# Moving 56 DMA issues from SyncE's queue to GpSimd's in a one-core hybrid decoder layer

## The chip, the cores and the metric

The kernel runs on one core of one Trainium2 chip. The metric is the device time of one execution in microseconds (us). Two times occur below: the median of three timed runs, and the time of the one execution that the profiler recorded, whose span runs from its first to its last instruction.

## What is computed

One layer is applied to 2048 new prompt tokens and to 8 single-token samples with saved states. In short form:

```
n    = rmsnorm(x)
proj = n @ w_in                      # u_s5 | q,k,v | z | beta, a
y    = gelu(s5_scan(u_s5))           # diagonal state space
gl   = y @ w_glu
y_s5 = gl[:, :512] * sigmoid(gl[:, 512:])          # the output gate
o    = delta_rule(l2norm(silu(conv(q,k,v))), ...)  # 4 delta net heads of 128
y_gdn = rmsnorm(o) * silu(z)
x = x + concat(y_s5, y_gdn) @ w_out
x = x + conv_ffn(rmsnorm(x))         # 1024 -> 2*2816 -> 1024
```

All matmuls of the large products are float32 split in a high and a low part, three products each.

## The kernel before

The 2048 prompt tokens are taken in four quarters of 512 columns (`QT`); quarter 0 also carries the 8 samples as columns 512 to 519. The stages follow each other loosely: norm and the S5 input products, then the S5 batches with the first delta net heads (list `MIXERS`), then from about 510 us the list `FFN`, in which the output gate (`s5_glu`), the rest of the delta net heads, the sample states and the four FFN quarters are interleaved letter by letter. TensorE runs its queue in order through all of it.

The tensor `mixT` in DRAM collects the results of both mixers, 1024 rows by 2056 columns. Rows 0 to 511 are written by the output gate (tile `mo`), rows 512 to 1023 by the heads (tile `zs`, end of `gdn_back`), the samples' columns by small stores. `ffn_mix` loads them again (tile `mr`), eight tiles for each quarter, and splits them into `nT`, the operand of the product with `w_out`; `ffn_res` loads the residual (tile `xr`).

`s5_glu` is called for quarters 0 and 1 and then for 2 and 3. For each of its two quarters it loads four tiles `yr` from `yD` (128 rows, each of 8 pieces of 64 floats) and, in quarter 0, a strip of 8 columns from `ysD`. ScalarE and VectorE split each into `yT`. Then four row blocks `a` follow, each with a weight load, two products, a sigmoid in `sg` and the gated result in `mo`, which is stored to `mixT`.

Three things set the order around these transfers. Each engine's queue is in order, and a DMA issue waits in the queue of the engine that issues it. SyncE (SP) issues nearly all loads and stores: the weights (`wr`, two buffers), the mixers' transfers, the bounce of `gdn_inverse` through `nD` and `xD`. GpSimd (POOL) issues the S5 results (`yD`, `ysD`), the output rows (`yout`), the sample states (`S0s`) and the samples' delta net result (`mixT<-sst`, line 1038), and computes the halos, the low parts of `gt` and the sums of squares. And `yr`, `sg`, `mo`, `zs`, `raw`, `t`, `s`, `mr`, `xr` and others share one pool of nine buffers (`NV = 9`, tag `v`), so a buffer whose store has not landed holds back the next tile of that pool.

The order of each queue is not the order of the source text. It is written at build time by a planner that plays the program through a timeline and gives each instruction a place when it could start there:

```python
TCARGS = dict(schedule_with_timeline_sim=True)
```

Of the kernel before, what the change touches and what calls it, by code (L numbers as in the profile page):

```python
# [20 lines left out]
QT = 512  # L21
NQ = QT + 8
# [35 lines left out]
def ncols(q):  # L58
    return NQ if q == 0 else QT


def blocks(q):
    return [(0, 256), (256, NQ)] if q == 0 else [(0, QT)]
# [6 lines left out]
def split(nc, hi, lo, raw, eng=None):  # L70

    nc.scalar.activation(hi, raw, AF.Copy)  # L72
    (eng or nc.vector).tensor_tensor(lo, raw, f32(hi), op=OP.subtract)  # L73


def sigmoid_(nc, out, x, scale=1.0):

    nc.scalar.activation(out, x, AF.Exp, scale=-scale)
    nc.scalar.activation(out, out, AF.Ln, bias=1.0)
    nc.scalar.activation(out, out, AF.Exp, scale=-1.0)  # L80
# [13 lines left out]
def rsqrt_cols(c, ss, n, scale, tag, rows=128, tmp=None):  # L94

    a, y, t = tmp or [c.sm.tile([128, n], F32, name=tag + s) for s in ("_a", "_y", "_t")]
    a, y, t = a[:rows], y[:rows], t[:rows]
    c.nc.vector.tensor_scalar(a, ss, scale, c.epscol[:rows], op0=OP.mult, op1=OP.add)
    return rsqrt_(c.nc, a, y, t)
# [185 lines left out]
def mm3(nc, out, wh, wl, xh, xl, first, last):  # L285
    nc.tensor.matmul(out, lhsT=wh, rhs=xh, start=first, stop=False)  # L286
    nc.tensor.matmul(out, lhsT=wh, rhs=xl, start=False, stop=False)  # L287
    nc.tensor.matmul(out, lhsT=wl, rhs=xh, start=False, stop=last)  # L288


def wsplit(c, src, eng=None):

    hi, lo, wr = c.W("whi"), c.W("wlo"), c.WR("wr")
    src(wr)
    split(c.nc, hi, lo, wr, eng or c.wl)
    return hi, lo
# [421 lines left out]
def s5_glu(c, q0, yT):  # L718

    nc = c.nc  # L720
    Q = (q0, q0 + 1)
    for i, q in enumerate(Q):
        for kt in range(4):
            rows = slice(kt * 128, kt * 128 + 128)
            yr = c.V("yr")
            nc.sync.dma_start(yr[:, :QT].rearrange("p (j m) -> p j m", j=8), c.yD[rows, :, q * 64:(q + 1) * 64])
            if q == 0:
                nc.sync.dma_start(yr[:, QT:NQ], c.ysD[rows])
            n = ncols(q)
            split(nc, yT[:, 4 * i + kt, 0, :n], yT[:, 4 * i + kt, 1, :n], yr[:, :n])  # L730
    wg = c.inp["s5_w_glu"][0].rearrange("(k p) f -> p k f", p=128)
    for a in range(4):
        v = lambda t: t.rearrange("p (k s f) -> p k s f", k=4, s=2)

        def load(wr):
            for s in range(2):
                nc.sync.dma_start(v(wr)[:, :, s], wg[:, :, s * 512 + a * 128:s * 512 + a * 128 + 128])
        h4, l4 = (v(t) for t in wsplit(c, load))
        for i, q in enumerate(Q):
            sg, mo = c.V("sg"), c.V("mo")  # L740
            for (b0, b1) in blocks(q):
                pab = {}
                for s in (1, 0):
                    p = pab[s] = c.ps("mm")
                    for kt in range(4):
                        K = 4 * i + kt
                        mm3(nc, p[:, :b1 - b0], h4[:, kt, s], l4[:, kt, s], yT[:, K, 0, b0:b1], yT[:, K, 1, b0:b1], kt == 0, kt == 3)
                    if s == 1:
                        sigmoid_(nc, sg[:, b0:b1], p[:, :b1 - b0])
                pa = pab[0]  # L750
                n8 = min(b1, QT) - b0
                j0, j1 = b0 // 64, (b0 + n8) // 64
                nc.vector.tensor_tensor(mo[:, 0:QT].rearrange("p (m j) -> p j m", j=8)[:, j0:j1],
                                        pa[:, :n8].rearrange("p (j m) -> p j m", m=64),
                                        sg[:, b0:b0 + n8].rearrange("p (j m) -> p j m", m=64), op=OP.mult)
                if b1 > QT:
                    nc.vector.tensor_tensor(mo[:, QT:NQ], pa[:, n8:n8 + 8], sg[:, QT:NQ], op=OP.mult)
            nc.sync.dma_start(c.mixT[a * 128:(a + 1) * 128, q * QT:(q + 1) * QT], mo[:, 0:QT])
            if q == 0:
                nc.sync.dma_start(c.mixT[a * 128:(a + 1) * 128, 2048:2056], mo[:, QT:NQ])  # L760
        yield


# [186 lines left out]
def gdn_back(c, q, h, col, F):  # L950

    nc, gp, sm = c.nc, c.gp, c.sm
    S0 = c.Sst[:, h]
    kq, kg, vt, AT, hc, zs, T = F
    ot = gp.tile([128, QT], F32, name="ot", bufs=1).rearrange("p (a b) -> p a b", a=4)
    for ci in range(4):
        sl = slice(ci * 128, ci * 128 + 128)
        pV = c.ps("b")
        nc.tensor.matmul(pV[:, 0:128], lhsT=kq[:, 0, sl], rhs=S0, start=True, stop=True)
        nc.tensor.matmul(pV[:, 128:256], lhsT=kq[:, 1, sl], rhs=S0, start=True, stop=True)  # L960
        rv = gp.tile([128, 128], F32, name="rv", bufs=1)
        nc.vector.scalar_tensor_tensor(rv, pV[:, 0:128], col[:, 6, ci, h:h + 1], vt[:, ci], op0=OP.mult, op1=OP.add)
        nc.scalar.activation(ot[:, ci], pV[:, 128:256], AF.Copy, scale=col[:, 3, ci, h:h + 1])
        nc.tensor.matmul(pV[:, 256:384], lhsT=T[:, ci], rhs=rv, start=True, stop=True)
        vn = gp.tile([128, 128], F32, name="vn", bufs=1)
        nc.vector.tensor_scalar(vn, pV[:, 256:384], hc[:, 5, ci:ci + 1], None, op0=OP.mult)
        pO = c.ps("b")
        nc.tensor.matmul(pO[:, 0:128], lhsT=kg[:, ci], rhs=vn, start=True, stop=True)
        nc.tensor.matmul(pO[:, 128:256], lhsT=AT[:, ci], rhs=vn, start=True, stop=True)
        nc.vector.scalar_tensor_tensor(S0, S0, col[:, 5, ci, h:h + 1], pO[:, 0:128], op0=OP.mult, op1=OP.add)  # L970
        nc.vector.tensor_tensor(ot[:, ci], pO[:, 128:256], ot[:, ci], op=OP.add)

    so = sm.tile([128, 4], F32, name="so")
    for ci in range(4):
        jk = gp.tile([128, 128], F32, name="jk2", tag="rv", bufs=1)
        nc.scalar.activation(jk, ot[:, ci], AF.Square, accum_out=so[:, ci:ci + 1])
    nc.vector.tensor_tensor(so, so, hc[:, 6], op=OP.mult)
    f = rsqrt_cols(c, so, 4, 1.0, "ro")
    nc.vector.tensor_tensor(f, f, hc[:, 1], op=OP.mult)
    for ci in range(4):  # L980
        nc.scalar.activation(ot[:, ci], ot[:, ci], AF.Copy, scale=f[:, ci:ci + 1])
    po = c.ps("b")
    for ci in range(4):
        nc.tensor.transpose(po[:, ci * 128:(ci + 1) * 128], ot[:, ci], c.ident)
    nc.vector.scalar_tensor_tensor(zs[:, :QT], po, c.col1(C_ON), zs[:, :QT], op0=OP.mult, op1=OP.mult)
    nc.sync.dma_start(c.mixT[512 + h * 128:512 + h * 128 + 128, q * QT:(q + 1) * QT], zs[:, :QT])


def gdn_sample(c, col):
# [301 lines left out]
def kernel(tc, inp, outp):  # L1291
# [7 lines left out]
    with ExitStack() as es:  # L1299
# [114 lines left out]
        def rest():  # L1414
            x2 = c.fb.tile([128, 8, NQ], F32, name="x2")
            nT = c.fb.tile([128, 8, 2, NQ], F32R, name="nT2")
            for q0 in (0, 2):
                yield from s5_glu(c, q0, nT)
            xrs, fin = ffn_mix(c, 0, nT), lambda: None
            yield  # L1420
            for q in range(4):
                xrs, fin = yield from ffn(c, q, x2, nT, xrs, fin)
# [35 lines left out]
```

## Time and profile before

| what | value |
|---|---|
| median of three runs | 2814.07 us (2813.53 to 2818.86) |
| the profiled execution's own time | 2812.3 us |
| its span | 2810.5 us |
| TensorE (PE) busy, weight loads (PEld) | 95%, 81% |
| VectorE, ScalarE, GpSimd busy | 76%, 50%, 24% |
| mean granted TensorE clock | 0.975 |
| DMA, hardware queue and software queue | 283.27 MB and 28.61 MB |

The shares are of the span. The execution's own time is 1.8 us longer than the span, and 1.8 us shorter than the median. DMA issues, register and semaphore instructions do not count as busy. The hardware queue is that of SyncE's issues, the software queue that of GpSimd's.

### The profile page before, as it was taken

The page shows a single profiled execution, that of the slowest core. Times are in us where ns is not written, and L with a number is a line of the kernel's source. Part 1 is how long each engine was busy: PE and PEld are TensorE (multiplying, and loading weights), DVE is VectorE, ACT ScalarE, POOL GpSimd, SP SyncE. Part 2 cuts the span into 40 slices and gives each one's busy share as a digit, 9 for nine tenths or more (in the row PEclk, how much of TensorE's full clock was granted, in tenths as well). Part 3 has the DMA queues.
Part 4 walks back from the last instruction along what each step waited for, and adds up shares of the span by engine and source line. Part 5 has one row for each costly group of instructions (what it writes and reads, how often), then busy time and mean ns, then how long its engine had stood idle before and what let it go on. Part 6 is the DMA issues. An engine that isn't in the chain of part 4 may idle for free.

```text
span 2810.5 us, 43010 instructions
## 1 busy us (share of the span) xinstructions
PE 2669.6 (95%) x15216; PEld 2266.6 (81%) x15216; DVE 2134.4 (76%) x4726; ACT 1391.7 (50%) x2806; POOL 661.9 (24%) x940
## 2 busy tenths in 40 slices
PE   5988888899999999998999999999999998999998
PEld 4887776787988999998777878877888787788887
DVE  6678899767778887778598777986868677677776
ACT  4535665554555544444544554544544434444443
POOL 3325431000121122212331111213212222322223
PEclk9998888999999999999999999999999999999999
DMA  7654433454434332333434333344333334443432
GB/s 198 201 155 117 123 104 109 103 129 117 117 85 108 86 96 85 95 92 111 126 97 121 90 92 106 85 133 125 95 100 90 91 93 133 141 119 99 123 116 69
DMA packets 421674, 314.63 MB, mean 112 GB/s; under 512 B 75311, under 2 KB 371672, under 8 KB 421443
## 3 DMA queue, kind: packets, MB, share of 16 engines
q1 hardware_dynamic: 411123, 283.27, 35.2%
q0 software_dynamic: 10336, 28.61, 3.4%
q8 instruction: 120, 1.97, 0.3%
q14 instruction: 95, 0.78, 0.1%
HBM read 264.74 MB, written 47.34 MB: 111 GB/s over the span
## 4 chain that ended last, share of the span: by engine, by line
PE 76%; DVE 13%; DMA 5%; issue 3%; ACT 2%; SPq 1%; POOL 0%; POOLq 0%; ACTq 0%; DVEq 0%
PE psmm L286 17%; PE psmm L287 17%; PE psmm L288 17%; PE psd L286 5%; PE psd L287 5%; PE psd L288 5%; DVE hh L654 1%; DVE wlo L73 1%; DVE tm L911 1%; DVE x L1107 1%; DVE nT L73 1%; DVE x L1197 1%; DVE X L912 1%; PE psf L887 1%; DMA N<-nD 1%
## 5 line engine op out<-in xcount | busy, mean ns | idle before, releaser
L286 PE MATMUL psmm<-nT,whi 128*128 128x512 f32 (+2 forms) x2992 | 1067.3, 358 | 29.8 <-ACT zs L841 8.0
L287 PE MATMUL psmm<-nT,whi 128*128 128x512 f32 (+2 forms) x2992 | 1060.4, 355 | 1.3 <-DVE nT L223 0.8
L288 PE MATMUL psmm<-nT,wlo 128*128 128x512 f32 (+2 forms) x2992 | 1058.0, 354 | 0.4 <-POOL wlo L73 0.4
L72 ACT ACTIVATE whi<-wr 128x1024 fp32r<-128x1024 f32 x372 | 394.0, 1060 | 608.5 <-PE psmm L287 443.9
L286 PEld LDWEIGHTS psmm<-nT,whi 128*128 128x128 f32 x2992 | 569.9, 191 | 109.9 <-ACT zs L841 8.7
L287 PEld LDWEIGHTS psmm<-nT,whi 128*128 128x128 f32 x2992 | 570.4, 191 | 79.1 <-issue 1.7
L288 PEld LDWEIGHTS psmm<-nT,wlo 128*128 128x128 f32 x2992 | 569.8, 191 | 78.9 <-issue 0.9
L73 DVE TENSOR_TENSOR wlo<-wr,whi 128x1024 fp32r<-128x1024 f32 x356 | 445.6, 1253 | 92.4 <-ACT whi L72 89.9
L1107 DVE TENSOR_TENSOR x<-psd,x 128x512 f32<-128x512 f32 (+2 forms) x464 | 257.1, 557 | 144.4 <-PE psd L288 142.6
L286 PE MATMUL psd<-gt,whi 128*128 128x512 f32 (+2 forms) x928 | 323.5, 349 | 16.5 <-DVE x L1107 14.5
L287 PE MATMUL psd<-gt,whi 128*128 128x512 f32 (+2 forms) x928 | 317.2, 342 | 0.0
L288 PE MATMUL psd<-gt,wlo 128*128 128x512 f32 (+2 forms) x928 | 315.3, 341 | 0.0
L1254 DVE SCALAR_TENSOR_TENSOR t<-raw,cc,t 128x512 f32<-128x512 f32 x352 | 270.6, 771 | 14.2 <-ACT t L1251 6.6
L1255 POOL COPY halo<-raw 128x2 f32<-128x2 f32 x176 | 77.4, 440 | 777.9 <-DVE raw L1250 702.2
L286 PEld LDWEIGHTS psd<-gt,whi 128*128 128x128 f32 x928 | 175.2, 189 | 47.2 <-DVE x L1107 22.0
L73 POOL TENSOR_TENSOR gt<-s,gt 128x512 fp32r<-128x512 f32 (+1 forms) x88 | 132.3, 1503 | 321.0 <-ACT gt L72 320.7
L287 PEld LDWEIGHTS psd<-gt,whi 128*128 128x128 f32 x928 | 175.4, 189 | 21.7
L288 PEld LDWEIGHTS psd<-gt,wlo 128*128 128x128 f32 x928 | 174.8, 189 | 20.8
L1250 DVE TENSOR_TENSOR raw<-psmm,rs 128x512 f32<-128x512 f32 (+1 forms) x214 | 123.7, 578 | 67.4 <-PE psmm L288 65.7
L1251 ACT ACTIVATE t<-raw,cc 128x512 f32<-128x512 f32 (+1 forms) x176 | 127.0, 722 | 64.6 <-DVE raw L1250 61.3
L911 DVE TENSOR_TENSOR tm<-X,N 128x124 f32<-128x124 f32 (+30 forms) x496 | 132.4, 267 | 28.9 <-DMA N<-nD 19.8
L1117 POOL TENSOR_TENSOR sq<-sq 128x256 f32<-128x256 f32 (+3 forms) x84 | 96.3, 1146 | 222.2 <-ACT sq L1115 219.6
(493 smaller groups left out, 3542.3 us busy)
## 6 DMA issues: line engine op xcount, KB each, us to landing
wr<-in_ffn_w_up_dram SPq DMA_DIRECT2D x176, 512.0 KB
wr<-in_ffn_w_down_dram SPq DMA_DIRECT2D x88, 512.0 KB
wr<-in_w_in_dram SPq DMA_DIRECT2D x64, 512.0 KB
wr<-in_w_out_dram SPq DMA_DIRECT2D x32, 512.0 KB
xTD<-xT SPq DMA_DIRECT2D x32, 256.0 KB
N<-nD SPq DMA_DIRECT2D x16, 512.0 KB
mr<-mixT SPq DMA_DIRECT2D x32, 256.0 KB
xr<-xTD SPq DMA_DIRECT2D x32, 256.0 KB
```

The source lines that it names most:

```text
L72: nc.scalar.activation(hi, raw, AF.Copy)
L73: (eng or nc.vector).tensor_tensor(lo, raw, f32(hi), op=OP.subtract)
L286: nc.tensor.matmul(out, lhsT=wh, rhs=xh, start=first, stop=False)
L287: nc.tensor.matmul(out, lhsT=wh, rhs=xl, start=False, stop=False)
L288: nc.tensor.matmul(out, lhsT=wl, rhs=xh, start=False, stop=last)
L911: nc.vector.tensor_tensor(m, X[:, :, j:j + 1].to_broadcast(sh), N[:, j:j + 1, j + 1:].to_broadcast(sh), op=OP.mult)
L1107: nc.vector.tensor_tensor(x2[:, j, b0:b1], p, x2[:, j, b0:b1], op=OP.add)
L1117: c.nc.gpsimd.tensor_tensor(acc[0], acc[0], s, op=OP.add)
L1250: nc.vector.tensor_tensor(raw[:, 2 + b0:2 + b1], p, rsB[:, b0:b1], op=OP.mult)
L1251: nc.scalar.activation(t[:, :n], raw[:, 2:2 + n], AF.Copy, scale=w[2])
L1254: nc.vector.scalar_tensor_tensor(t[:, :QT], raw[:, j:j + QT], w[j], t[:, :QT], op0=OP.mult, op1=OP.add)
L1255: nc.gpsimd.tensor_copy(c.halo[:, ch], raw[:, QT:QT + 2])
```

## The change

The issues of four kinds of transfers, and of the small strips that go with two of them, are made by GpSimd. These are 16 loads of `yr` from `yD` with 4 strips from `ysD`, 16 stores of `mo` with 4 strips, and 16 stores of `zs`. Sizes, tiles, buffers and the computing instructions stay as they are.

```diff
             yr = c.V("yr")
-            nc.sync.dma_start(yr[:, :QT].rearrange("p (j m) -> p j m", j=8), c.yD[rows, :, q * 64:(q + 1) * 64])
+            nc.gpsimd.dma_start(yr[:, :QT].rearrange("p (j m) -> p j m", j=8), c.yD[rows, :, q * 64:(q + 1) * 64])
             if q == 0:
-                nc.sync.dma_start(yr[:, QT:NQ], c.ysD[rows])
+                nc.gpsimd.dma_start(yr[:, QT:NQ], c.ysD[rows])
...
-            nc.sync.dma_start(c.mixT[a * 128:(a + 1) * 128, q * QT:(q + 1) * QT], mo[:, 0:QT])
+            nc.gpsimd.dma_start(c.mixT[a * 128:(a + 1) * 128, q * QT:(q + 1) * QT], mo[:, 0:QT])
             if q == 0:
-                nc.sync.dma_start(c.mixT[a * 128:(a + 1) * 128, 2048:2056], mo[:, QT:NQ])
+                nc.gpsimd.dma_start(c.mixT[a * 128:(a + 1) * 128, 2048:2056], mo[:, QT:NQ])
...
-    nc.sync.dma_start(c.mixT[512 + h * 128:512 + h * 128 + 128, q * QT:(q + 1) * QT], zs[:, :QT])
+    nc.gpsimd.dma_start(c.mixT[512 + h * 128:512 + h * 128 + 128, q * QT:(q + 1) * QT], zs[:, :QT])
```

## Rows read from the trace of the kernel before

**Rows 1.** Windows by stage: length, busy time (count) of each engine, clock, DMA.

```profile
422.00:510.00 88.00, 74.72 (x405) 56.69 (x404) 78.77 (x246) 52.83 (x143) 19.33 (x28) 0.84 0.37 105
510.00:700.00 190.00, 178.74 (x1054) 150.08 (x1054) 127.10 (x410) 99.94 (x255) 7.98 (x17) 0.94 0.45 117
700.00:2810.00 2110.00, 2064.75 (x11477) 1750.68 (x11477) 1605.80 (x3166) 1016.73 (x1852) 476.19 (x712) 0.99 0.36 104
```

**Rows 2.** Waits of TensorE: us in total, times, longest.

```profile
PE psmm L286 <- ACT whi L72: 4.8, 3, 3.5
...
PE psd L286 <- ACT whi L72: 1.5, 1, 1.5
...
PE psf L1003 <- DMA S0s<-in_state_gdn_dram: 0.6, 1, 0.6
```

**Rows 3.** Waits in SyncE's queue (SPq), same columns.

```profile
SPq L986 <- DVE zs L985: 43.3, 10, 13.4
...
SPq L758 <- DVE mo L753: 22.5, 5, 6.0
```

**Rows 4.** DMA issues by tile: ns min/median/max, first and last start, last S0s' landing.

```profile
L726 SPq DMA_DIRECT2D yr<-yD x16: 517/546/969, 514.7 to 623.4; - x16
...
L728 SPq DMA_DIRECT2D yr<-ysD x4: 642/650/650, 515.3 to 523.9; - x4
...
L758 SPq DMA_DIRECT2D mixT<-mo x16: 319/328/534, 539.1 to 688.7; - x16
...
L986 SPq DMA_DIRECT2D mixT<-zs x16: 319/338/345, 422.2 to 2357.5; - x16
...
L1220 POOL DMA_DIRECT2D out_dram<-yout x34: 513/540/583, 1339.3 to 2806.3; - x34
...
L996 POOL DMA_DIRECT2D S0s<-in_state_gdn_dram x4: 882/892/929, 613.9 to 627.4; - x4
...
DMA to landing us min/median/max: 3.8/5.3/8.6
```

**Rows 5.** DMA issues of the page: count, KB each, median us to landing.

```profile
out_dram<-yout POOLq DMA_DIRECT2D x32, 256.0 KB, 3.6
```

**Rows 6.** Timeline of SyncE's queue: start, us, line, transfer, count.

```profile
514.70 0.58 SPq L726 DMA_DIRECT2D yr<-yD  x1
...
609.25 3.31 SPq L726 DMA_DIRECT2D yr<-yD  x4
...
683.57 0.45 SPq L1129 DMA_DIRECT2D mr<-mixT  x1
688.65 0.32 SPq L758 DMA_DIRECT2D mixT<-mo  x1
689.02 0.42 SPq L1127 DMA_DIRECT2D mr<-mixT  x1
```

**Rows 7.** Chain that ended last, in order of time: start, us, what.

```profile
515.33 2.81 DMA yr<-ysD
...
520.32 3.55 DMA yr<-ysD
...
613.90 4.73 DMA S0s<-in_state_gdn_dram
...
756.55 4.60 DMA xr<-xTD
```

**Rows 8.** Timeline of TensorE; in brackets the idle time before and what ended it.

```profile
519.01 0.80 PE L286 MATMUL psmm<-nT,whi 128*128 128x256 f32 x2 [1.02 <-ACT nT L72]
...
700.56 0.50 PE L286 MATMUL psmm<-nT,whi 128*128 128x512 f32 x1 [1.89 <-ACT t L825]
...
761.72 0.38 PE L286 MATMUL psmm<-nT,whi 128*128 128x256 f32 x1 [1.55 <-DVE x L1153]
```

**Rows 9.** Windows, sum over sixteen stretches of 10 us that hold zs stores after 700.

```profile
sum 160.00, PE 156.96 PEld 136.63 DVE 117.67 ACT 82.59 POOL 35.81; mean PE 9.81 PEld 8.54 DVE 7.35 ACT 5.16 POOL 2.24
```

**Rows 10.** Timeline of GpSimd's queue, the wait in front of line 1038.

```profile
681.90 0.77 POOL L1038 DMA_DIRECT2D mixT<-sst  x1 [53.65 <-DVE sst L1037]
```

## The prediction, made before the changed kernel was run

> **What bounds the kernel now.** I read the windows by stage first, because the transfers that move all lie behind 422 us: the first `zs` store is issued there and the last at 2357.5 [rows 4]. From 422 to 510 TensorE is busy 74.72 of 88 us, from 510 to 700 (the output gate) 178.74 of 190, from 700 on 2064.75 of 2110 [rows 1]. So 13.3 + 11.3 + 45.3 = 69.9 us of idle TensorE time is all that the change can give back in its stretch, and TensorE work itself is untouched by it. The granted clock is 0.94 in the gate's stage and 0.99 afterwards [rows 1], so there is little in the clock either.
>
> Next come the waits, to see which idle time hangs on DMA. TensorE's waits for a split weight are 4.8 and 1.5 us in all, and it waits 0.6 us for a sample state [rows 2]. SyncE's queue, in contrast, stands 43.3 us in front of `zs` stores and 22.5 us in front of `mo` stores [rows 3]; weight loads are queued behind these. The two views together are the point of this case: SyncE waits a lot, and TensorE almost never notices, since the weights are split ahead of their use.
>
> Then I followed the four places where a moved transfer, or one queued behind it, ends a TensorE wait: the gate's entrance at 515, the sample states at 614, the gate's end at 689 and a residual load at 756 [rows 6 to 8].
>
> **Issue time.** SyncE loses 16 x 0.546 + 4 x 0.65 for `yr`, 16 x 0.328 + 4 x some 0.35 for `mo`, and 16 x 0.338 for `zs`: about 23 us [rows 4]. GpSimd gains them at its own prices. A `yr` load has 128 rows of 8 pieces, as an `S0s` load has, so I take that issue's 0.892 us; a `mo` or `zs` store has 128 plain rows of 2 KB like `yout`, so 0.540 us; for the eight strips also 0.54. That is 14.3 + 17.3 + 4.3 = 36 us. Most of it (some 28 us) falls in the stage in which GpSimd computes 7.98 of 190 us [rows 1], the rest is eleven issues spread over 2110 us of which GpSimd fills 476. That idle time is the cover. Without it each issue would put 0.5 to 0.9 us in front of a halo or a `gt` split. I take 0 for TensorE.
>
> **The entrance of the gate, 515 us.** On SyncE the first `yr` is issued at 514.70 and its strip has landed at 515.33 + 2.81 = 518.14, which is 3.44 us after the first issue [rows 6, 7]. The first products wait for its split, with 1.02 us of TensorE idle [rows 8], and the second pair (520.32 + 3.55) is again on the chain [rows 7], because its buffer comes free late. On GpSimd the nearest row above is the first `S0s` load, which has as many pieces and twice the bytes: 4.73 us [rows 7], so 1.3 us later. The nearest below is a 256 KB `yout` store at 3.6 us [rows 5], 0.2 us later. The pieces are what a `yr` load shares with `S0s`, so I take 1.3 us, twice: +2.6. The bounds are 0 and twice 8.6 - 3.44 us (the slowest of the later `S0s` transfers [rows 4]), about +10.
>
> The Trainium skill, "DMA: Bandwidth & Descriptors", section "Latency and other measured facts", gives a first byte after about 1 us for a GpSimd issue and about 0.6 us for a SyncE issue, which speaks against the change. By it alone the term would be an estimated 2 x 0.4 = +0.8 us in place of +2.6, and the sum below would be 1.8 us lower. No row here separates a first byte from the rest of a transfer.
>
> **The sample states, 614 us.** The second half of the gate issues four `yr` loads at 609.25 [rows 6], and the first `S0s` is issued at 613.90 from the other queue [rows 7]. TensorE waits 0.6 us for it [rows 2], so a later landing is paid in full. After the change the `S0s` data stand behind four `yr` (1.05 MB) in one queue. The 4.73 us of the first 512 KB is 111 GB/s for one queue that shares the engines; two of these were issued together, so up to twice that, 222 GB/s, passed. At 222 GB/s 1.05 MB takes 4.7 us; issued from 609.25 on and with some 1.3 us until data move they are through at about 615.3, 1.4 us after the `S0s` issue, and GpSimd's longer issue of the four (3.6 against 3.31 us) adds 0.3. I take +1.7. The lower bound is 0, if `S0s` is queued first; the upper is all eight `yr` in front, 2.1 MB or +9.4 us.
>
> **The end of the gate, 689 us.** The load of the second `mr` stands in SyncE's queue behind the last `mo` store: the strip before it ends at 684.02, then SyncE waits until 688.65 for `mo` and issues `mr` at 689.02 [rows 6]. ScalarE's splits of these `mr` sit in front of the evacuation of a head's product, and TensorE idles 1.89 us on that at 700.56 [rows 8]. With `mo` in GpSimd's queue, the `mr` loads of quarter 0 can go up to 4.6 us earlier: they need the `mo` of quarter 0 and not the last one. The wait is at most 1.89 us, so -1.9, at worst 0. What is late next is the `mr` buffer itself, which is one of the shared nine.
>
> **The residual at 756 us.** The store of a `zs` holds an `xr` load in SyncE's queue; that load's 4.60 us is on the chain [rows 7] and TensorE idles 1.55 us for it at 761.72 [rows 8]. Moved, it gives up to -1.55, at worst 0.
>
> **The other `zs` stores.** Sixteen stretches around the eleven stores after 700 us show 156.96 of 160 us TensorE busy [rows 9], and half of the missing 3 us is the 1.55 just counted. The last store, at 2357.5, is followed by an `mr` load that depends on it; TensorE has other products then. I take 0 for all, and for the earlier ones too.
>
> **The sum.** 0 + 2.6 + 1.7 - 1.9 - 1.55 = +0.85 us on the profiled execution's own 2812.3, or 2813.2; the median stands 1.8 us above that execution, so 2815 us. The bounds of the four terms alone are -3.5 and +19.
>
> **What the sum leaves out.** The planner writes new queues for all engines from 422 us on, because it times the two issuers differently. The trace of before can't show that order. I take 0 and keep both signs in the rivals.
>
> **Rivals.** *Everything moved is hidden anyway*: the planner keeps TensorE's order and slots cover the later landings; 2814 us. Rows 9 and the small waits of rows 2 speak for it, the two `yr` on the chain [rows 7] against. The Trainium skill, same page, section "Issuing engines are not separate DMA queues", says that issuing from several engines saves only sequencer time, since all run on the same 16 DMA engines; that speaks for this rival.
>
> *Faster, SyncE's queue is what counts*: the 43.3 and 22.5 us of waits [rows 3] no longer hold weights back, all of TensorE's 6.3 us of weight waits [rows 2] go, with the 1.9 and 1.55 above, and the entrance stays covered: -9.8, or 2804 us. Against it: at most 6.3 us of 69.9 hang on weights.
>
> *Slower, a blocked GpSimd queue*: line 1038 holds GpSimd 53.65 us until 681.90 [rows 10]. If it is queued ahead of `mo` stores, each keeps one of the nine shared buffers. Up to four held ones leave enough for `sg`, `mo` and a head's tiles; from the fifth on TensorE runs out, at about 660 us, and stands until 682: +20, or 2834 us. Against it: the planner places an instruction when it could start, and the `mo` are ready earlier.
>
> *Slower, a worse order of the gate and heads*: at the idle share of the stretch before it (13.3 of 88 us [rows 1]) the gate's 190 us would hold 28.7 us of idle instead of 11.3; half of that loss is +8.7, or 2823 us, all of it 2831.
>
> **How the numbers follow.** About 0.2% (5.6 us) is what a measurement of this kernel can tell from no change. The forecast of the sum has 0.30 and the hidden case 0.12, together 0.42 within 0.2%. The freed SyncE queue has 0.25 (faster). The worse order, with the upper bounds of the entrance and of `S0s`, has 0.23 and the blocked queue 0.10, together 0.33 slower. Cases of both signs hold more than half, so the likeliest one's own range is 2809 to 2820; for 8 in 10 it reaches to 2803, just past the freed queue's time, and to 2831, which leaves out the blocked queue and some of either tail.
>
> **What would show it.** Right: GpSimd's issues near 0.9 us for `yr` and 0.54 for the stores; the first `yr` landing 4 to 5 us after its issue; TensorE idle in the gate's stage between 10 and 17 us and its waits at 700 and 761 gone; SyncE's waits for `zs` and `mo` gone and standing in GpSimd's queue. Wrong: a GpSimd wait of tens of us in front of a `mo` store, `raw` or `gt` waiting behind one, or more than 5 us of change in TensorE's idle time after 700, where no moved transfer but `zs` is left; that would be the order and not a transfer.

## The result, and the profile after

The changed kernel takes 2833.29 us in the median (2830.66 to 2836.17), beside 2816.47 us (2813.53 to 2819.46) for the kernel before on the same chip. The ratio is 1.006, with a 95% interval of 1.0048 to 1.0072: 17 us slower, outside the forecast range of 2803 to 2831. The profiled execution's own time is 2836.17 us, its span 2834.4 us, 23.9 us longer than the span of before.

The windows by stage, with the same columns as [rows 1], put the loss in the gate's stage:

```profile
422.00:510.00 88.00, 74.66 (x430) 58.01 (x429) 78.96 (x245) 53.90 (x148) 18.36 (x26) 0.86 0.38 107
510.00:700.00 190.00, 168.11 (x988) 140.71 (x986) 118.12 (x398) 92.32 (x237) 36.76 (x57) 0.90 0.37 103
700.00:2834.00 2134.00, 2090.04 (x11564) 1772.10 (x11562) 1620.55 (x3189) 1029.43 (x1873) 481.48 (x728) 0.99 0.36 105
```

TensorE idles 21.9 us between 510 and 700, where it idled 11.3 us, and the clock there is 0.90 instead of 0.94. Windows of fixed times hold different work in the two kernels, so I cut both traces at the same work. The borders are the first group of sample-state products, the last `mo` store, the last `zs` store and the end; TensorE executes 381 and 382 matmuls in the first piece. First the kernel before:

```profile
618.80:688.70 69.90, 68.38 (x381) 57.34 (x382) 45.91 (x147) 31.32 (x69) 2.53 (x3) 0.93 0.43 117
688.70:2357.50 1668.80, 1635.02 (x9536) 1402.83 (x9535) 1297.76 (x2704) 820.71 (x1552) 346.12 (x545) 0.99 0.36 103
2357.50:2810.50 453.00, 439.70 (x1988) 355.81 (x1986) 314.81 (x472) 201.93 (x310) 130.60 (x169) 0.99 0.38 114
```

Then the changed kernel:

```profile
625.70:710.60 84.90, 73.73 (x382) 60.99 (x383) 45.16 (x147) 33.24 (x71) 11.88 (x18) 0.86 0.45 124
710.60:2378.70 1668.10, 1639.15 (x9536) 1407.01 (x9535) 1298.08 (x2704) 820.87 (x1551) 348.67 (x557) 0.99 0.35 102
2378.70:2834.40 455.70, 440.39 (x1986) 356.58 (x1985) 317.11 (x472) 202.38 (x310) 131.50 (x170) 0.99 0.38 113
```

One piece carries the loss: 84.90 us for what took 69.90. Of these 15.0 us, 9.65 are idle TensorE time (11.17 against 1.52 us) and 5.35 are longer matmuls (73.73 against 68.38 us busy, at a clock of 0.86 against 0.93). The other pieces differ by -0.7 and +2.7 us. The rest of the 23.9 us, 6.9 us, lies ahead of the piece: the first `yr` is issued 4.5 us later (519.18 against 514.70), most of the way to it without any moved transfer (the first is at 422 us), and the way from it to the first `mo` store is 2.6 us longer.

Inside the piece there is one large wait. TensorE's timeline (idle time before an instruction in brackets):

```profile
638.54 0.39 PE L288 MATMUL psmm<-nT,wlo 128*128 128x512 f32 x1
648.75 0.80 PE L959 MATMUL psb<-Sst,kq 128*128 128x128 f32 x2 [9.82 <-DVE ot L971]
```

TensorE waits for the state and output updates of a running delta net head (lines 970, 971), which VectorE (DVE in the rows) makes. VectorE's timeline shows why they are late:

```profile
632.73 0.69 DVE L73 TENSOR_TENSOR nT<-yr,nT 128x512 fp32r<-128x512 f32 x1 [0.29 <-ACT nT L72]
645.57 0.29 DVE L911 TENSOR_TENSOR tm<-X,N 128x124 f32<-128x124 f32 x1 [12.15 <-DMA N<-nD]
...
647.36 0.34 DVE L970 SCALAR_TENSOR_TENSOR Sst<-Sst,col,psb 128x128 f32<-128x128 f32 x1
...
648.41 0.29 DVE L971 TENSOR_TENSOR ot<-psb,ot 128x128 f32<-128x128 f32 x1
```

The first product of the next head's inverse (line 911, the sixth of 16 inverses) stands ahead of them in VectorE's queue and waits 12.15 us for the tile `N`. This tile makes a trip through DRAM: `gdn_inverse` writes four 16 KB blocks to `nD` (line 902) and reads them back as the 512 KB of `N` (line 904). Both are issued by SyncE, and neither is part of the change. The chain that ended last runs through both:

```profile
627.49 8.90 DMA nD<-LT
...
636.54 9.01 DMA N<-nD
```

In the kernel before, the four blocks were issued at 619.28 and `N` at 624.10, 4.8 us later; here 626.13 and 636.54, 10.4 us apart. And in VectorE's queue of before the first product stood behind the head's updates:

```profile
637.59 0.35 DVE L970 SCALAR_TENSOR_TENSOR Sst<-Sst,col,psb 128x128 f32<-128x128 f32 x1 [1.74 <-PE psb L969]
637.85 0.28 DVE L971 TENSOR_TENSOR ot<-psb,ot 128x128 f32<-128x128 f32 x1
638.05 0.28 DVE L911 TENSOR_TENSOR tm<-X,N 128x124 f32<-128x124 f32 x1
```

What travels beside the trip is seen in GpSimd's queue of the changed kernel:

```profile
615.97 0.54 POOL L760 DMA_DIRECT2D mixT<-mo  x1
620.76 1.79 POOL L996 DMA_DIRECT2D S0s<-in_state_gdn_dram  x2 [4.25 <-PE psmm L288]
622.54 3.50 POOL L726 DMA_DIRECT2D yr<-yD  x4
626.03 0.57 POOL L758 DMA_DIRECT2D mixT<-mo  x1
626.59 0.89 POOL L726 DMA_DIRECT2D yr<-yD  x1
```

The second half's `yr` stand behind two sample states, which wait 4.25 us for TensorE. They went 0.9 us after the `mo` store before them (608.32 and 609.25 [rows 6]), and now go 7.1 us after it (615.43), in one burst with the states. The shares of the two queues in the DMA engines follow (queue: packets, MB, share of 16 engines), first for 628 to 636.5 us, then 636.5 to 640, then 640 to 645.6:

```profile
q0 software_dynamic: 660, 2.23, 98.8%
q1 hardware_dynamic: 576, 0.07, 6.3%
...
q0 software_dynamic: 256, 0.86, 101.2%
q1 hardware_dynamic: 1, 0.00, 0.6%
...
q1 hardware_dynamic: 143, 0.52, 43.2%
q0 software_dynamic: 59, 0.18, 14.9%
```

All of `N` (143 packets, 0.52 MB) moves after 640 us, when the software queue has run down; in the 3.5 us after its issue one packet of the hardware queue passed. In the kernel before, the hardware queue had 89.4% of the engines in 621 to 624, the software queue 5.9%.

### The profile page after: what moved, and what is told of

It is laid out like the page before. It is cut to its first block, busy times and chain, and to the rows that moved or that the text cites. A ratio compares the mean times of both kernels' runs of the same rounds, so it can differ in the third digit from the quotient of the medians.

```text
span 2834.4 us, 43024 instructions
## 1 busy us (share of the span) xinstructions
PE 2677.1 (94%) x15216; PEld 2271.9 (80%) x15216; DVE 2135.6 (75%) x4726; ACT 1394.4 (49%) x2806; POOL 694.4 (25%) x996
## 4 chain that ended last, share of the span: by engine, by line
PE 76%; DVE 13%; DMA 5%; ACT 3%; issue 2%; SPq 1%; POOL 0%; POOLq 0%; DVEq 0%; ACTq 0%
PE psmm L286 18%; PE psmm L287 17%; PE psmm L288 17%; PE psd L286 5%; PE psd L287 5%; PE psd L288 5%; DVE hh L654 1%; DVE wlo L73 1%; DVE tm L911 1%; DMA N<-nD 1%; DVE x L1107 1%; DVE nT L73 1%; DVE X L912 1%; ACT whi L72 1%; DMA nD<-LT 1%
```

## The experiments

**Theory.** The second half's `yr`, late and in one burst with the sample states on the software queue, slow the trip of `nD` and `N` on the hardware queue (A). The planner has put VectorE's first product ahead of the head's updates, so TensorE pays for it (B). Both are needed. **Rivals:** the `mo` or `zs` stores, which hold shared buffers longer; the order alone; any single part of the `yr` change.

### Each kind of transfer alone

Each of these kernels is the kernel before with one or two of the diff's parts. First the `yr` loads and their strips:

```diff
-            nc.sync.dma_start(yr[:, :QT].rearrange("p (j m) -> p j m", j=8), c.yD[rows, :, q * 64:(q + 1) * 64])
+            nc.gpsimd.dma_start(yr[:, :QT].rearrange("p (j m) -> p j m", j=8), c.yD[rows, :, q * 64:(q + 1) * 64])
             if q == 0:
-                nc.sync.dma_start(yr[:, QT:NQ], c.ysD[rows])
+                nc.gpsimd.dma_start(yr[:, QT:NQ], c.ysD[rows])
```

> Only the yr loads and their strips move to GpSimd, the stores of mo and zs stay with SyncE. Theory A (the yr loads, queued with the S0s loads, delay a head's bounce nD, N through DRAM, and TensorE stands for it): all of the change's loss is here, +14 to +20 us over before (about 2830 to 2836), with a TensorE wait of 7 us or more for a delta net instruction between 620 and 660 us, and N landing 15 us or more after nD's issue. Theory B (stores waiting in GpSimd's queue hold the shared buffers): less than +6 us here.

Measured: 2833.89 us, ratio 1.0057 (1.0044 to 1.007). The whole loss is here, within the interval. Its trace has the same slow trip (`N` lands 18.6 us after the first `nD` issue) and a wait of the same kind, of 5.96 us where 7 or more was expected; what stood behind the product on VectorE was one more split of the gate's input, and the timelines of VectorE and TensorE read:

```profile
639.85 0.29 DVE L911 TENSOR_TENSOR tm<-X,N 128x124 f32<-128x124 f32 x1 [6.80 <-DMA N<-nD]
...
642.52 0.79 PE L287 MATMUL psmm<-nT,whi 128*128 128x512 f32 x1 [5.96 <-DVE nT L73]
```

Then the stores, alone and together:

```diff
-            nc.sync.dma_start(c.mixT[a * 128:(a + 1) * 128, q * QT:(q + 1) * QT], mo[:, 0:QT])
+            nc.gpsimd.dma_start(c.mixT[a * 128:(a + 1) * 128, q * QT:(q + 1) * QT], mo[:, 0:QT])
...
-    nc.sync.dma_start(c.mixT[512 + h * 128:512 + h * 128 + 128, q * QT:(q + 1) * QT], zs[:, :QT])
+    nc.gpsimd.dma_start(c.mixT[512 + h * 128:512 + h * 128 + 128, q * QT:(q + 1) * QT], zs[:, :QT])
```

> Only the mo stores move to GpSimd. Theory A: between -3 and +2 us; the gate ends at the same place, and the TensorE wait of 1.89 us behind the gate (mr loads queued behind the last mo store) is gone. Theory B: +8 us or more, with tiles of the shared pool (sg, raw, yr) waiting for mo's landing.

> Only the sixteen zs stores move to GpSimd. Theory A and the prediction's own term: between -2 and +1 us; the TensorE wait of 1.55 us at the xr load near 761 us is gone. Theory B: +3 us or more, spread over the FFN, with gt splits and halo copies late behind zs stores in GpSimd's queue.

> Both kinds of stores move, the yr loads stay with SyncE. Theory A: -4 to +1 us against before, 2811 to 2818. Theory B: most of the +17 us is here, 2828 or more.

Measured: `mo` 1.0001 (0.9992 to 1.001), `zs` 0.9991 (0.9982 to 0.9999), both 0.9993 (0.9983 to 1.0003). The stores cost nothing and give next to nothing, and the rival of held buffers falls.

### Which half of the yr loads

The function is called with `q0` 0 for the first half and 2 for the second. The kernel before, with the first half's loads (and its strips) on GpSimd:

```diff
-            nc.sync.dma_start(yr[:, :QT].rearrange("p (j m) -> p j m", j=8), c.yD[rows, :, q * 64:(q + 1) * 64])
+            (nc.sync if q0 else nc.gpsimd).dma_start(yr[:, :QT].rearrange("p (j m) -> p j m", j=8), c.yD[rows, :, q * 64:(q + 1) * 64])
             if q == 0:
-                nc.sync.dma_start(yr[:, QT:NQ], c.ysD[rows])
+                nc.gpsimd.dma_start(yr[:, QT:NQ], c.ysD[rows])
```

And with the second half's alone:

```diff
-            nc.sync.dma_start(yr[:, :QT].rearrange("p (j m) -> p j m", j=8), c.yD[rows, :, q * 64:(q + 1) * 64])
+            (nc.gpsimd if q0 else nc.sync).dma_start(yr[:, :QT].rearrange("p (j m) -> p j m", j=8), c.yD[rows, :, q * 64:(q + 1) * 64])
```

> Of the gate's input loads, only those of the first half of the tokens (8 yr and 4 strips ysD) are issued by GpSimd; the second half's yr, the mo and the zs stay on SyncE. Theory (the second half's yr in one burst with the sample states on GpSimd's queue slow the inverse's trip through DRAM): only the entrance term, some 2 to 4 us above before, 2818 to 2821, nD and N land within 3 us as before, and DVE's first product of the sixth inverse waits under 2 us for N. Rival (any yr on GpSimd's queue, by the order of the work that follows): 10 us or more above before, 2827 or later.

> The complement: only the second half's 8 yr are issued by GpSimd, the first half's and the strips, the mo and the zs by SyncE. Theory: these loads stand behind the sample states in GpSimd's queue and come in one burst with them, so nD and N take 8 to 9 us each and TensorE stands 6 to 10 us behind DVE; 10 to 15 us above before, 2827 to 2832. Rival (the entrance, the first half's, carries the loss): under 4 us above before.

Measured: first half 1.0009 (0.9998 to 1.0021), some 2.5 us; second half 1.0042 (1.0026 to 1.0057), some 12 us. With the first half alone `N` is issued 5.6 us after the first `nD` block and VectorE never waits for it. With the second half alone the wait is back (TensorE's is 5.47 us, where 6 to 10 was expected), in VectorE's timeline:

```profile
640.68 0.29 DVE L911 TENSOR_TENSOR tm<-X,N 128x124 f32<-128x124 f32 x1 [6.78 <-DMA N<-nD]
```

### The order on VectorE

The changed kernel, with one edge of order for the planner: the first product of the sixth inverse behind the 18th output update of all. `behind` counts the inverses in `c.ninv` and adds an order that needs no semaphore, since both instructions run on VectorE.

```diff
+    behind = lambda c, i, n, k: c.ninv.append(0) or len(c.ninv) == n + 1 and c.tc.add_manual_dep(i, c.ots[k].name, mybir.DependencyInfo(mybir.DependencyClass.NoSync, mybir.DependencyReason.DATA), reason='order')
...
-        nc.vector.tensor_tensor(m, X[:, :, j:j + 1].to_broadcast(sh), N[:, j:j + 1, j + 1:].to_broadcast(sh), op=OP.mult)
+        i = nc.vector.tensor_tensor(m, X[:, :, j:j + 1].to_broadcast(sh), N[:, j:j + 1, j + 1:].to_broadcast(sh), op=OP.mult); j == 0 and c.behind(i.ins, 5, 17)
...
-        nc.vector.tensor_tensor(ot[:, ci], pO[:, 128:256], ot[:, ci], op=OP.add)
+        c.ots.append(nc.vector.tensor_tensor(ot[:, ci], pO[:, 128:256], ot[:, ci], op=OP.add).ins)
```

> The changed kernel, with one order given by hand: DVE's first product of the sixth inverse (L911, which needs N) is queued behind the output update of the running head's fifth chunk group (L971), as it stands in the kernel before; every issue stays on GpSimd. Theory: N still lands late (nD and N 8 us or more each), but no instruction that TensorE needs stands behind it on DVE, so the stall of 9.8 us before L959 goes and the kernel recovers at least 8 of the 17 us: 2821 to 2825. Rival (the loss is spread over the gate's stage by GpSimd's queue, and the place of one instruction is a symptom): under 4 us recovered, 2829 or later.

Measured: 2823.09 us, ratio 1.0016 (1.0003 to 1.0029): 0.0044 of 0.0060 come back, some 12 us, although the trip is no faster. The chain and VectorE's timeline:

```profile
631.41 10.62 DMA nD<-LT
642.16 7.70 DMA N<-nD
```

```profile
640.53 0.35 DVE L970 SCALAR_TENSOR_TENSOR Sst<-Sst,col,psb 128x128 f32<-128x128 f32 x1 [3.19 <-PE psb L969]
...
649.88 0.29 DVE L911 TENSOR_TENSOR tm<-X,N 128x124 f32<-128x124 f32 x1 [0.69 <-DMA N<-nD]
```

The trip from the first `nD` issue (630.00) to the landing of `N` (649.86) takes 19.9 us, against 19.4 in the changed kernel (626.13 to 645.55), and VectorE waits 0.69 us, because it has the head's and the gate's work in the meantime. In the gate's stage TensorE has no wait above 0.68 us then. The counterpart is the kernel before with the opposite order, the 17th output update behind that product:

```diff
+    behind = lambda c, i, n, k: c.ninv.append(0) or len(c.ninv) == n + 1 and c.tc.add_manual_dep(c.ots[k], i.name, mybir.DependencyInfo(mybir.DependencyClass.NoSync, mybir.DependencyReason.DATA), reason='order')
...
+        i = nc.vector.tensor_tensor(m, X[:, :, j:j + 1].to_broadcast(sh), N[:, j:j + 1, j + 1:].to_broadcast(sh), op=OP.mult); j == 0 and c.behind(i.ins, 5, 16)
```

> The kernel before, all issues on SyncE, with the opposite order given by hand: the output update of the running head's chunk (L971, the 17th of all) is queued on DVE behind the first product of the sixth inverse (L911), about as the changed kernel has it. Theory (both are needed, a late N and DVE standing for it ahead of the head): N is prompt here, so DVE stands under 2 us for it and the time stays within 0.2% of before. Rival (the order alone is the loss): 8 us or more above before.

Measured: 1.0001 (0.9988 to 1.0014). The output update went from 0.3 us behind its state update to 6 us behind it, and nothing was lost:

```profile
633.06 0.35 DVE L970 SCALAR_TENSOR_TENSOR Sst<-Sst,col,psb 128x128 f32<-128x128 f32 x1 [4.90 <-PE psb L969]
...
639.31 0.28 DVE L911 TENSOR_TENSOR tm<-X,N 128x124 f32<-128x124 f32 x1
639.51 0.28 DVE L971 TENSOR_TENSOR ot<-psb,ot 128x128 f32<-128x128 f32 x1
```

The test is weaker than meant: the planner left the first product at 639.31, 11.6 us after the issue of `N` (627.68), and VectorE did not stand for it. It shows that the order costs nothing with `N` on chip, not what it would cost with `N` asked for at 633. So that the order needs a late `N` to cost anything is shown for this one place of the product only.

### Why the trip is slow

The changed kernel with the sample states issued by SyncE, and the changed kernel with the first of them queued behind the first four `yr`:

```diff
-    load = lambda t, h: nc.gpsimd.dma_start(t, c.inp["state_gdn"][0][:, h].rearrange("b d e -> d b e"))
+    load = lambda t, h: nc.sync.dma_start(t, c.inp["state_gdn"][0][:, h].rearrange("b d e -> d b e"))
```

> The changed kernel, with the four loads of the sample states (S0s, L996) issued by SyncE instead of GpSimd, so that nothing of theirs stands ahead of the second half's yr in GpSimd's queue and none of their bytes travel on it. Theory A (head-of-line and burst with the sample states): yr of the second half issue from about 614 instead of 622, nD and N land in 2 to 4 us, and 8 us or more of the 17 come back: 2821 to 2825. Rival (yr on the software queue alone slow nD and N, whatever goes with them): nD and N stay at 8 us or more each and under 4 us come back.

(`c.yrs` collects the 16 `yr` issues, `c.s0` those of the states; the one edge of order is between the first state and the twelfth `yr`.)

```diff
-        load(S0, h)
+        c.s0.append(load(S0, h).ins); len(c.s0) == 1 and len(c.yrs) > 11 and c.behind(c.s0[0], c.yrs[11])
```

> The changed kernel with one order in GpSimd's queue: the first load of the sample states (S0s, L996) is queued behind the first four yr of the second half, instead of ahead of them. All issues stay on GpSimd. Theory (head of line: in the changed kernel the yr stand behind S0s, whose own wait lets them go only at 622 us, into the same microseconds as nD and N): the four yr go at about 611 us and have landed before nD, N is on chip within 5 us of its issue, and 8 us or more of the 17 come back: 2821 to 2825. Rival (anything on the software queue beside nD and N slows them, at whatever time the first four go, since the last four and the sample states still go beside them): N's trip stays at 8 us or more; then the time hangs on what stands behind the first product on DVE, and half or more of the loss stays: 2826 or later.

Measured: 1.0024 (1.0014 to 1.0034) and 1.0029 (1.0017 to 1.004). Of the 0.0060 they give back 0.0036 and 0.0031, some 10 and 9 us. That is the 8 us or more of the theory, but the trip that it named (`N` on chip in 4 or 5 us) is not there in either run. With the states on SyncE, two of them (1 MB) were issued at 624.00, right ahead of `N` at 627.97, and `N` took 9.53 us behind them; that run moved the obstacle into the trip's own queue. VectorE stood 7.67 us for `N` in it, and yet TensorE has no wait above 1.04 us in the gate's stage: what it lost there (6.9 us by the table below) is 4.9 us of longer matmuls and 2.0 us of idle time. Soon after the first sample-state products start (621.02) it ran at the lower clock for 9 us:

```profile
621.90:630.90 9.00, 9.00 (x36) 8.32 (x37) 3.09 (x6) 2.24 (x5) 2.65 (x3) 0.50 1.00 254
```

With the four `yr` first, they went at 616.96, 1.1 us after the `mo` store ahead of them (615.90), and the chain has

```profile
627.95 3.84 DMA nD<-LT
631.94 6.50 DMA N<-nD
```

So the blocks are 5 us faster when the four `yr` start earlier; `N`, which still runs beside the last `yr` and, from 636.00 on, one state, is 2.5 us faster. VectorE waits 4.97 us for it, TensorE 4.22 us. With this order 7.6 of the 17.9 us go that the two pieces of the trip take in the changed kernel; 10.3 us are left. The edit moved more than the four `yr`: the last two states went at 636.00 and 643.07 instead of 628.03 and 632.41, so the run does not tell the place of the `yr` from a thinner burst beside the trip. At the next head of the kernel before, the chain has 1.53 us for `nD`.

What is left might come from the size of what shares the engines. The 16 loads and 4 strips are 17,216 packets on a hardware queue and 1,408 on the software queue: the counts of the hardware queue differ by 17,216 between the kernel before (411,123) and the one with `yr` alone (393,907), those of the software queue by 1,408 (10,336 and 11,744). Their 4.21 MB make some 3 KB a packet there, beside the 128-byte rows of `nD`. To test this, ScalarE issues the same loads, on a second hardware queue:

```diff
-            nc.sync.dma_start(yr[:, :QT].rearrange("p (j m) -> p j m", j=8), c.yD[rows, :, q * 64:(q + 1) * 64])
+            nc.scalar.dma_start(yr[:, :QT].rearrange("p (j m) -> p j m", j=8), c.yD[rows, :, q * 64:(q + 1) * 64])
```

> The gate's input loads (16 yr, 4 strips) are issued by ScalarE instead of SyncE; mo and zs stay on SyncE. They leave SyncE's queue as in the change, but do not travel on the software queue: the profile should count them as some 17,000 small packets of a hardware queue again, not as 1,400 of about 3 KB. Theory (the large packets of the software queue, taken turn by turn with the 128-byte packets of nD, make nD take 8 to 9 us): nD lands in under 4 us after its first issue, N likewise, DVE stands under 2 us for N, and the kernel is within 5 us of before, the cost of the issues on ScalarE's own queue included. Rival (any transfers on a second queue beside nD and N slow them, whatever their packets): nD and N take 7 us or more each.

Measured: 2830.43 us, ratio 1.0026 (1.0015 to 1.0038), some 7 us over the kernel before where the theory of packet sizes allowed 5. It missed, and on the trip too. SyncE's queue:

```profile
620.38 5.30 SPq L902 DMA_DIRECT2D nD<-LT  x4
630.62 0.53 SPq L904 DMA_DIRECT2D N<-nD  x1
```

`N` is issued 10.2 us after the first block, as late as in the changed kernel. From 625 to 630.6 us ScalarE's queue (q10), the software queue and SyncE's (q1) had:

```profile
q10 hardware_dynamic: 3473, 0.88, 78.3%
q0 software_dynamic: 144, 0.52, 32.8%
q1 hardware_dynamic: 554, 0.07, 8.8%
```

The `yr` are small packets here, but a sample state passed beside the trip in some 3.6 KB a packet, so the run did not take large packets away from it. Part of the delay has another source, since the issues of the four blocks alone took 5.30 instead of 1.83 us, and three `yr` issues on ScalarE 6.34 us. VectorE's order was that of before here, it did not wait (the product at 641.89 followed the update at 641.68). By the pieces below, the profiled execution lost 3.5 us in the gate and 6.5 us behind it, in a stretch without any of the moved loads. There TensorE's idle time is 2.3 us shorter and its busy time 8.8 us longer for the same 9536 matmuls (1643.83 against 1635.02 us); why was not followed up. Large packets of the `yr` are not needed for a slow issue of `N`; whether large packets are what slows the trip in the changed kernel stays open.

### Both losses undone

The changed kernel with the first half's `yr` back on SyncE and with the order on VectorE:

```diff
-            nc.gpsimd.dma_start(yr[:, :QT].rearrange("p (j m) -> p j m", j=8), c.yD[rows, :, q * 64:(q + 1) * 64])
+            (nc.gpsimd if q0 else nc.sync).dma_start(yr[:, :QT].rearrange("p (j m) -> p j m", j=8), c.yD[rows, :, q * 64:(q + 1) * 64])
             if q == 0:
-                nc.gpsimd.dma_start(yr[:, QT:NQ], c.ysD[rows])
+                nc.sync.dma_start(yr[:, QT:NQ], c.ysD[rows])
...
+        i = nc.vector.tensor_tensor(m, X[:, :, j:j + 1].to_broadcast(sh), N[:, j:j + 1, j + 1:].to_broadcast(sh), op=OP.mult); j == 0 and c.behind(i.ins, 5, 17)
```

> The changed kernel with its two losses undone: the first half's yr and strips go back to SyncE, and DVE's first product of the sixth inverse is queued behind the head's output update (L971), as in the run with that order alone. The second half's yr, the mo and the zs stay on GpSimd. Theory (entrance some 2.5 us, order some 12 us, nothing else): 2813 to 2818, within 0.2% of before; if the waits that left at 700 and 756 us counted, 2811 to 2813. Rival (late N costs more than its place in DVE's queue): 2820 or later.

Measured: 2823.49 us beside 2820.47 us for the kernel before on the same chip, ratio 1.0008 (0.9998 to 1.0018): within 0.2% of the kernel before, as the theory has it; not faster. The expected 2813 to 2818 us was not met, because the kernel before took more there; by its time alone (2820 or later) the rival would have come true. No version here is clearly faster than the kernel before.

### The pieces of all runs

The profiled executions can be compared by piece, from the starts of three issues in SyncE's, GpSimd's and ScalarE's timelines. The time to the first `yr` differs from one execution to the next by up to 9 us (514.33 to 523.11) and says nothing of an edit.

| kernel | first `yr` to first `mo` store | first to last `mo` store | last `mo` to last `zs` store |
|---|---|---|---|
| before | 24.44 | 149.51 | 1668.8 |
| `mo` alone | 24.72 | 149.52 | 1669.1 |
| `zs` alone | 24.82 | 149.98 | 1669.1 |
| `mo` and `zs` | 24.64 | 149.67 | 1670.1 |
| `yr` first half | 28.18 | 149.73 | 1670.4 |
| `yr` second half | 24.79 | 163.49 | 1667.1 |
| `yr` alone | 27.98 | 161.53 | 1670.6 |
| after | 27.02 | 164.40 | 1668.1 |
| after, order on VectorE | 27.13 | 153.91 | 1671.1 |
| after, states on SyncE | 27.30 | 156.44 | 1668.9 |
| after, four `yr` first | 27.49 | 157.51 | 1668.8 |
| `yr` on ScalarE | 24.65 | 153.05 | 1675.3 |
| both undone | 24.89 | 152.11 | 1668.6 |
| before, opposite order | 24.74 | 150.76 | 1672.1 |

The columns separate cleanly. The first is 2.6 to 3.7 us longer wherever the first half's `yr` are on GpSimd, and nowhere else. The second is 12.0 to 14.9 us longer where the second half's stand behind the states on GpSimd and the order is the planner's, and 6.9 to 8.0 us where they don't stand behind them. The order on VectorE takes 10.5 of the 14.9 us back, and 2.6 to 4.4 us stay in the three runs with a late `N` for which VectorE does not stand. Of these, 1.8 to 2.8 us are longer TensorE time (147.53 to 148.53 us busy against 145.77) and the rest is idle time; what makes it longer was not tested.

## Why the prediction was wrong

**What bounds the kernel.** Right in its place: the two pieces that lost, 2.6 and 14.9 us, lie between 510 and 711 us. The bound of 69.9 us of idle time limited the gain and not the loss. That there is little in the clock was wrong for the loss: 5.35 of the 15.0 us of the piece are the same matmuls taking longer, at 0.86 instead of 0.93.

**Issue time.** Right: 0.883 us in the median for `yr` (0.892 taken), 0.540 for `mo`, 0.558 for `zs`, and no cost in TensorE's time for the stores (0.9993).

**The entrance, +2.6.** Right in size, by luck: 27.02 against 24.44 us is +2.6, and the first half alone measured some 2.5. But the two strips were not 1.3 us later each. ScalarE's first two splits start 4.11 and 10.06 us after the first `yr` issue (523.29 and 529.24), against 3.62 and 9.25 us before, so 0.5 and 0.8 us later, and the next two are not later at all. TensorE's idle time on the way to the first `mo` store is 4.85 against 4.43 us; its busy time is 22.17 against 20.01 us, at a clock of 0.74 against 0.79, with two groups of a head's products (lines 877 and 887) ahead of the quarter's 264-column products, where they came behind most of them before. Which of these makes the 2.6 us was not tested.

**The sample states, +1.7: the step that failed.** It asked how late `S0s` lands behind four `yr`, and gave 0 as the lower bound "if `S0s` is queued first". It is queued first, and that is the bad case. The states wait 4.25 us for TensorE, the `yr` behind them go 6 us later, and both then run beside a third transfer that I did not price: the trip of `nD` and `N` on SyncE's queue, issued from 619.28 to 627.8 in the kernel before, which no part of the diff touches. I asked what would be late next on the queue that gained work and not on the queue that shares the DMA engines with it. What the term itself names did not happen: TensorE waits 0.64 us for the first state (0.56 before). The loss in its place, the wait for `N`, is 14.9 us (164.40 against 149.51 us) where the sum had 1.7.

**What the sum leaves out: the planner's order, taken as 0.** The second half of the same failure. The order is worth 10.5 of the 14.9 us, since with it changed by hand the late `N` costs 4.4. The planner put the first product where it stands 12 us for `N`; the trace of before shows the other order.

**The gate's end and the residual, -1.9 and -1.55.** The two waits are gone: from 697 to 795 us TensorE has none above 0.72 us. The one at 700 is gone with `mo` alone and stays (1.99 us) with `zs` alone; the one at 762 is gone with `zs` alone and stays (1.12 us) with `mo` alone, as the two terms have it. The time is not back: from the last `mo` to the last `zs` store it is 1668.1 against 1668.8 us, and 1670.1 in the run with both stores moved. The rows of that piece show where it went. TensorE's idle time fell by 4.8 us (1668.10 - 1639.15 against 1668.80 - 1635.02), more than the two terms, and the same 9536 matmuls took 4.1 us longer. Part of that goes with the granted clock: the changed kernel has two stretches of 8 us at a mean of 0.79 (from 922.6 and from 2366.6) where the kernel before, 22 us earlier, has 1.00. A wait that goes need not be worth its length.

**The rivals.** The worse order of gate and heads (2823 to 2831 us) has the right place. Its price came from the idle share of another stage and says nothing of the mechanism. The blocked GpSimd queue was the nearest in time, with 2834 us, by luck: it did not happen. Line 1038 waits 5.09 us, with all but two `mo` stores ahead of it. The freed SyncE queue did not pay: with `mo` and `zs` moved, the waits in front of them leave SyncE, and the time is 0.9993. The hidden case holds for 32 of the 48 large transfers and not for `yr`.

**What would show it.** The prices of the issues were seen as said. Idle time of 10 to 17 us in the gate's stage was to show me right; it is 21.9. None of the signs that I gave for being wrong names a wait for `N`.

The Trainium skill, "DMA: Bandwidth & Descriptors", section "Issuing engines are not separate DMA queues", says that issuing from another engine saves only the issuing sequencer's time. The runs agree for the stores (0.9993). They add that it can cost much more than that time, here 14.9 us, since it changes what stands ahead of a transfer, beside which others it runs, and what the planner puts where. The same page, section "Queues, rings and completion order", says that each DMA engine takes turns between queues, a packet at a time. By this rule the small packets of `nD` would pay for every large one beside them, if what the profile counts as a packet is the page's packet, which no run here shows. In 632 to 634 us of the changed kernel 324 packets of the hardware queue passed with 169 of the software queue, in 13.6% and 89.0% of the engines' time, which agrees in direction and not one for one. The single packet in the 3.5 us after `N`'s issue is not explained by it.

## What to carry to other kernels

When issues move to another engine's queue, look first at what they will stand behind there, and then at which transfers of untouched queues fall into the same microseconds; the loss here is in a transfer that the diff does not name. On an in-order engine, an instruction that waits for a DMA sets the price of that DMA by what is queued behind it: the late tile cost 14.9 us ahead of a head's update and 4.4 us behind it. When a planner writes the order, a change of issuers can change the queue of an engine that issues none of them, as it did VectorE's here, so compare the queues of the two builds before believing a sum over single transfers.

## What the hardware showed beyond that

The same load pattern (128 rows of 8 pieces of 256 bytes) counted as some 3 KB a packet on the software queue and as 256-byte packets on a hardware queue: 1,408 and 17,216 packets for the same 4.21 MB.

With the `yr` on ScalarE's queue, issues took longer on both queues: the four of `nD` 5.30 us on SyncE (1.83 in the kernel before), and three of `yr` 6.34 us on ScalarE (2.72 on SyncE before, at 621.20). Why was not tested.

TensorE paid twice for its wait. Behind the 9.82 us without work it ran at a granted clock of 0.50, the 1.2 GHz level, for some 7 us, as these windows of the changed kernel show, and was back at 1.00 (2.4 GHz) by 656.2. The first row is a stretch at 0.50 before the wait; 32 sample-state products in a row (from 625.71 on) had run just ahead of it:

```profile
629.00:635.00 6.00, 6.00 (x18) 5.03 (x19) 3.03 (x5) 2.19 (x4) 3.52 (x4) 0.50 1.06 281
648.80:650.00 1.20, 1.20 (x6) 1.20 (x7) 0.89 (x4) 0.00 (x0) 0.00 (x0) 0.50 0.00 0
650.00:652.00 2.00, 2.00 (x11) 2.00 (x11) 1.89 (x7) 1.40 (x3) 0.00 (x0) 0.50 0.00 0
652.00:655.50 3.50, 3.50 (x13) 3.11 (x14) 1.67 (x6) 2.10 (x3) 0.57 (x1) 0.50 0.19 75
656.20:660.00 3.80, 3.80 (x27) 3.41 (x26) 2.34 (x10) 0.00 (x0) 0.00 (x0) 1.00 0.00 0
```

The kernel before had no such stretch there: 1.00 from 628.8 to 668.8 us. It had two elsewhere in the same piece, the first of them after 16 sample-state products (from 618.76 on):

```profile
621.00:623.50 2.50, 2.50 (x8) 2.02 (x9) 1.48 (x4) 1.35 (x3) 0.88 (x1) 0.50 0.91 184
675.00:681.00 6.00, 5.07 (x27) 4.33 (x28) 3.29 (x19) 3.40 (x10) 0.00 (x0) 0.50 0.06 13
```

At half of the full clock, some 7 us of work cost an estimated 3.6 us. With the 9.65 us of idle time that makes some 13 of the 15 us that the piece is longer. The rest is the balance of the other slow stretches, which was not worked out.
